# A hybrid transformer block on one core: the first half's small fp32 products become pairs of rounded products

## The chip, the cores and the metric

The kernel runs on one core of a Trainium2 chip. The metric is the device time of one execution, in microseconds; the time before is the median of three runs. A further execution was recorded by the hardware profiler, and everything said of engines, waits and single instructions comes from it.

## The reference

One layer of an encoder trunk for 256 tokens of width 2048, all in float32. Cut to what matters here:

```
u    = rms_norm(x) * g1
proj = u @ w_in                      # q,k,v of two attentions | r,k,v, low-rank inputs of RWKV-7 | three gates
y_a  = stick_breaking_attention      # 4 heads x 128: exp(log_beta + strictly later sums of log(1 - beta)) @ v
y_b  = forgetting_attention          # 4 heads x 128: softmax(q k / sqrt(d) + c[t] - c[s]) @ v, c = cumsum(log f)
y_c  = rwkv7_time_mix                # 16 heads x 64: decay and rate from low-rank products, normalised keys,
                                     # a recurrence over time, group norm, bonus sum(r k r_k) v, gate sigmoid(gd) @ g_up
m    = sum_i sigmoid(gate_i) * (y_i @ P_i)
x    = x + rms_norm(m @ w_out) * g2
x    = x + rms_norm(relu(rms_norm(x) @ w_up)^2 @ w_down) * g4
```

## The kernel before

**Rounded parts.** Weights and activations of the large products are each split in two: a high part in fp32r (a rounded float32, the type that the profile's rows name fp32r) and a low part, the value less the high part. ScalarE writes the high part (`whi`, L152) and VectorE the low one (`wlo`, L153) for each block of 128 x 1024 weights that SP's queue brings in; `split` does the same for an activation, into a tile `pk` of 512 columns, high and low side by side. A large product is then high weights by both activation parts, and low weights by the high part: L168, L172, L176 in `unit` and L198, L214 in `tok`. The small products of the attentions and of RWKV are done in plain fp32.

**Order.** TensorE's instructions stand in an order written out by hand for the first half of the kernel, up to the fourth block of the product with w_out. The main stream runs through the weights of w_in, of the branches and of w_out. Beside it run threads (`mixers`, `gate_norm`, `turns`), Python generators that yield the number of microseconds after which their next piece may be put in. `tick` counts the stream's time with 0.227 us per product of 512 columns and puts in what is due. So a yield decides behind which products of the stream a side product stands. The order on VectorE, ScalarE and POOL is chosen by a scheduler, which keeps each tile's dependences; each engine then works in that order. Tiles with the same tag share `bufs` buffers; a new tile waits until the last use of the one that it takes the place of.

**The threads.** `mixers` does the stick-breaking attention (`sb_mix`), the forgetting attention (`fox_mix`), the activation of the low-rank inputs (`rwkv_lora`) and two halves of RWKV with four head pairs each (`rwkv_half`). A half has these pieces: norm of the keys by a product with `bones`, the block matrix of ones (L543); for each head pair the low-rank products (L567, L569), the decay's running sum, the products within a chunk (L613), the bonus (L619); an inverse of 32 triangular 64 x 64 matrices on VectorE (31 steps, L657 and L659) and two products to finish it (L672, L679); and the passage over four chunks (L698 to L740). `gate_norm` then normalises the result with another product with `bones` (L766), an inverse root, and multiplies by the gate's low-rank product (L779, L780). Side products write to four psum banks `mps`, the stream to four banks `gps`.

**From the first half to the second.** After the product with w_out come the sums of squares of the result for both halves of the tokens (L969), the inverse root (`rstd_of`, L939 and L940 on POOL), the residual sum x1 (L956), its transposes (L988) and their split with a gain into the inputs of the up product (L233 on ScalarE, L234 on VectorE). The squares of x1 for the next norm are summed by ScalarE in `post` of the first eight units of the up product (L1113). `rstd_of` is used once more at the end of the kernel, ahead of the last sum (L1352) and the write of the output.

Of the kernel before, what the change touches and what calls it, by code (L numbers as in the profile page):

```python
# [50 lines left out]
def hybrid_block(ctx, tc, xt, x, gains, params, consts, lora, gup, wst, out):  # L51
# [264 lines left out]
    rstd = rp.tile([128, T], F32, tag="cs", name="rstd1", bufs=1)  # L316
# [41 lines left out]
    def sb_mix():  # L358
        yield "sb"
        q, k, v = done["sbq"], done["sbk"], done["sbv"]  # L360
        B = rp.tile([128, 2, 4, 384], F32, tag="SC", name="sbt", bufs=1)
        z, t = B[:, 0], B[:, 1]
        m0 = rp.tile([128, 4, 384], F32, tag="b6", name="sbm", bufs=1)
        for h in range(4):
# [11 lines left out]
        A.activation(t, t, AF.Ln, bias=1.0)  # L376
        for hp in range(2):
# [6 lines left out]
            yield 5.0 if hp == 0 else 8.0  # L384
        for hp in range(2):
            ps = mps()
            for i in range(2):
                h = 2 * hp + i
                PE.matmul(ps[:, i * 256:i * 256 + 256], C("trig"), z[:, h, 0:256], start=True, stop=False)
                PE.matmul(ps[:, i * 256 + 128:i * 256 + 256], C("ones"), z[:, h, 256:384], start=False, stop=True)  # L390
            V.tensor_tensor(m0[:, 2 * hp:2 * hp + 2, 0:256], ps.rearrange("p (a b) -> p a b", a=2),
                            t[:, 2 * hp:2 * hp + 2, 0:256], ALU.add)
            if hp == 0:
                yield 4.0
        ps = mps()
        PE.matmul(ps.rearrange("p (a b) -> p a b", a=4), C("trig"), z[:, :, 256:384], start=True, stop=True)
        V.tensor_tensor(m0[:, :, 256:384], ps.rearrange("p (a b) -> p a b", a=4), t[:, :, 256:384], ALU.add)
        yield 3.0
        for hp in range(2):
            hs = slice(2 * hp, 2 * hp + 2)  # L400
            A.activation(m0[:, hs], m0[:, hs], AF.Exp)
            for h in (2 * hp, 2 * hp + 1):
                for c in (0, 256):
                    G.tensor_tensor(m0[:, h, c:c + 128], m0[:, h, c:c + 128], C("mst"), ALU.mult)
            yield 2.0 if hp == 0 else 5.0
        out = []
        for h in range(4):
            ps = mps()
            PE.matmul(ps[:, 0:256], v[0][:, h * 128:h * 128 + 128], m0[:, h, 0:256], start=True, stop=False)
            PE.matmul(ps[:, 128:256], v[1][:, h * 128:h * 128 + 128], m0[:, h, 256:384], start=False, stop=True)  # L410
# [7 lines left out]
    def fox_mix():  # L418
# [16 lines left out]
        V.tensor_tensor_scan(lf, one, m0, 0.0, ALU.mult, ALU.add)  # L435
        yield 9.0
# [7 lines left out]
        for hp in range(2):  # L444
            ps = mps()
            for i in range(2):
                PE.matmul(ps[:, i * 256:i * 256 + 256],
                          C("ident", R, 32 + 2 * hp + i, 33 + 2 * hp + i).to_broadcast([4, 128]), lf,
                          start=True, stop=True)
# [58 lines left out]

    def rwkv_lora():
        yield "lora"  # L510
        xl, sy, zz = done["zx"], done["zy"], done["zz"]
        A.activation(xl[0:64], xl[0:64], AF.Tanh)
# [3 lines left out]
        yield 3.0  # L516

    def rwkv_half(hf):
        PR = range(4 * hf, 4 * hf + 4)
        xl, sy, sz = done["zx"], done["zy"], done["zz"]  # L520

# [5 lines left out]
        def lora_load(p):  # L527
            if p in PR:
                lor[p] = rp.tile([128, 128], F32, tag="lor", name=nm("lor"), bufs=2)
                nc.scalar.dma_start(out=lor[p], in_=lora[:, p * 128:p * 128 + 128])  # L530
# [6 lines left out]
        yield 2.6  # L537
        sq = []
        for i2 in range(2):
            ri = B6[:, 2 * i2:2 * i2 + 2, :]  # L540
            ps = mps()
            for i in range(2):
                PE.matmul(ps[:, i * T:i * T + T], C("bones"), rin[2 * i2 + i], start=True, stop=True)  # L543
# [19 lines left out]
        At, Bt, Kt, bon = {}, {}, {}, {}  # L563
        ecol = rp.tile([128, 4, 4], F32, tag="ecol", name=nm("ecol"), bufs=2)
        for i, p in enumerate(PR):
            ps = mps()
            PE.matmul(ps[:, 0:T], lor[p][0:64], xl[0:64], start=True, stop=True)  # L567
            ps2 = mps()
            PE.matmul(ps2[:, 0:T], lor[p][64:128], xl[64:128], start=True, stop=True)  # L569
            lora_load(p + 1)  # L570
            lw = rp.tile([128, T], F32, tag="lw", name=nm("lw"), bufs=1)
            c = rp.tile([128, T], F32, tag="cs", name=nm("cs"), bufs=1)
            th = rp.tile([128, T], F32, tag="tha", name=nm("tha"), bufs=1)
            em = rp.tile([128, T], F32, tag="em", name=nm("em"), bufs=1)
# [7 lines left out]
            A.activation(ep[:, :, 1:65], c4, AF.Exp)  # L582
            A.activation(em, c, AF.Exp, scale=-1.0)
# [20 lines left out]
            V.scalar_tensor_tensor(kp, r, P("rk", p), kp, ALU.mult, ALU.mult)  # L604
            yield f"v{p}"
# [13 lines left out]
            PE.matmul(psb[:, 0:T], C("bones"), kp, start=True, stop=True)  # L619
# [34 lines left out]
        for s in range(31):  # L654
# [5 lines left out]
            yield 0.6 + n * m * 4e-3  # L660
# [81 lines left out]
        start(gate_norm(hf, y, bon, sy, sz))  # L742

    def gate_norm(hf, y, bon, sy, sz):
        PR = range(4 * hf, 4 * hf + 4)
        gqs = {}

        def gup_load(p):
            if p in PR:
                gqs[p] = gq = rp.tile([128, 2, 128], F32, tag="gup", name=nm("gup"), bufs=2)  # L750
                G.memset(gq[:, 1, :], 0.0)
                nc.scalar.dma_start(out=gq[:, 0, :], in_=gup[0:128, 128 * p:128 * p + 128])
                nc.scalar.dma_start(out=gq[0:32, 1, :], in_=gup[128:160, 128 * p:128 * p + 128])

        gup_load(PR[0])
        var = rp.tile([128, 4, T], F32, tag="XT", name=nm("gn"), bufs=2)
# [722 lines left out]
```

## Time and profile before

| | |
|---|---|
| median of three runs | 1534.03 us (1532.95 to 1536.06) |
| profiled execution | 1534.53 us |
| its span, first to last instruction | 1532.8 us |
| mean granted clock of TensorE | 0.995 |
| TensorE's idle time within the span | 29.6 us |

The span lies 1.7 us below the time of the same execution. A line of the groups names the source line, the engine, the operation, the tiles and shapes, and the count; behind the bar stand the busy time in microseconds and the mean duration of one in nanoseconds, and then the idle time ahead of it with what ended it. A line of the timeline begins with the start and the time to the end of the group, both in microseconds. A window gives the busy time of TensorE, its weight loads, VectorE, ScalarE and POOL in that stretch, then the granted clock and the share of the DMA engines. Products overlap in TensorE's pipeline, so the duration of one is longer than its share of the engine's time.

### The profile page before, as it was taken

The page shows a single profiled execution, that of the slowest core. Times are in us where ns is not written, and L with a number is a line of the kernel's source. Part 1 is how long each engine was busy: PE and PEld are TensorE (multiplying, and loading weights), DVE is VectorE, ACT ScalarE, POOL GpSimd, SP SyncE. Part 2 cuts the span into 40 slices and gives each one's busy share as a digit, 9 for nine tenths or more (in the row PEclk, how much of TensorE's full clock was granted, in tenths as well). Part 3 has the DMA queues.
Part 4 walks back from the last instruction along what each step waited for, and adds up shares of the span by engine and source line. Part 5 has one row for each costly group of instructions (what it writes and reads, how often), then busy time and mean ns, then how long its engine had stood idle before and what let it go on. Part 6 is the DMA issues. An engine that isn't in the chain of part 4 may idle for free.

```text
span 1532.8 us, 22383 instructions
## 1 busy us (share of the span) xinstructions
PE 1503.2 (98%) x8294; PEld 1262.6 (82%) x8294; DVE 1192.7 (78%) x1608; ACT 917.8 (60%) x1340; POOL 91.0 (6%) x163
## 2 busy tenths in 40 slices
PE   7999999999999999999999999999999999999997
PEld 6888888888777788778888788888888888888885
DVE  6865567789548789447755868989899999899986
ACT  6664566554546553555444767777667776676753
POOL 0021000000000100000000000000000000000000
PEclk9999999999999999999999999999999999999998
DMA  7555445445534445535695657888888888888974
GB/s 259 192 166 166 164 165 181 165 150 183 182 111 150 165 152 184 175 124 179 208 322 187 231 181 222 249 263 239 262 253 258 242 254 270 249 246 264 260 247 151
DMA packets 105117, 316.88 MB, mean 207 GB/s; under 512 B 10288, under 2 KB 12720, under 8 KB 104624
## 3 DMA queue, kind: packets, MB, share of 16 engines
q1 hardware_dynamic: 93536, 282.76, 54.1%
q0 software_dynamic: 8064, 29.36, 10.3%
q10 hardware_dynamic: 3408, 3.34, 0.6%
q8 instruction: 65, 1.06, 0.3%
q14 instruction: 44, 0.36, 0.1%
HBM read 281.86 MB, written 4.19 MB: 187 GB/s over the span
## 4 chain that ended last, share of the span: by engine, by line
PE 53%; DVE 1%; DMA 1%; ACT 1%; issue 0%; POOL 0%; DVEq 0%; POOLq 0%; ACTq 0%
PE gps L168 14%; PE gps L214 10%; PE gps L172 8%; PE mps L1209 3%; PE mps L1210 3%; PE mps L1211 3%; PE gps L198 3%; PE gps L1211 2%; PE gps L1209 2%; PE gps L1210 2%; PE gps L176 1%; DMA sp<-in_wst_dram 1%; DVE x L1352 0%; DVE wlo L153 0%; ACT junk L1113 0%
## 5 line engine op out<-in xcount | busy, mean ns | idle before, releaser
L153 DVE TENSOR_TENSOR wlo<-raw,whi 128x1024 fp32r<-128x1024 f32 x507 | 616.0, 1222 | 192.2 <-ACT whi L152 174.8
L152 ACT ACTIVATE whi<-raw 128x1024 fp32r<-128x1024 f32 x507 | 533.9, 1057 | 276.0 <-PE gps L214 107.7
L168 PE MATMUL gps<-pk,whi 128*128 128x512 f32 x1301 | 330.9, 393 | 0.1
L214 PE MATMUL gps<-whi,pk 128*128 128x512 f32 x1144 | 291.5, 394 | 0.0
L168 PEld LDWEIGHTS gps<-pk,whi 128*128 128x128 f32 x1301 | 241.1, 188 | 48.4 <-issue 0.9
L214 PEld LDWEIGHTS gps<-whi,pk 128*128 128x128 f32 x1144 | 213.7, 188 | 45.8 <-issue 1.0
L172 PEld LDWEIGHTS gps<-pk,wlo 128*128 128x128 f32 x1391 | 190.1, 190 | 14.6 <-issue 1.2
L172 PE MATMUL gps<-pk,wlo 128*128 128x256 f32 x1391 | 195.8, 283 | 0.0
L214 PE MATMUL gps<-wlo,pk 128*128 128x512 f32 x572 | 157.4, 394 | 0.0
L214 PEld LDWEIGHTS gps<-wlo,pk 128*128 128x128 f32 x572 | 106.9, 188 | 23.2 <-issue 0.7
L1075 DVE TENSOR_TENSOR sp<-raw,sp 128x1024 fp32r<-128x1024 f32 x67 | 81.7, 1220 | 4.8 <-ACT sp L1074 4.6
L1074 ACT ACTIVATE sp<-raw 128x1024 fp32r<-128x1024 f32 x67 | 70.7, 1055 | 14.9 <-PE mps L1211 3.9
L1101 ACT ACTIVATE sp<-gps 128x512 f32<-128x512 f32 x52 | 31.1, 597 | 80.7 <-PE gps L176 80.7
L198 PE MATMUL gps<-whi,pk 128*128 128x512 f32 x264 | 71.9, 393 | 0.0
L1209 PE MATMUL mps<-whi,fm 128*128 128x512 f32 x168 | 66.2, 394 | 0.0
L1210 PE MATMUL mps<-whi,fm 128*128 128x512 f32 x168 | 65.8, 392 | 0.0
L1211 PE MATMUL mps<-wlo,fm 128*128 128x512 f32 x168 | 65.5, 390 | 0.0
L1171 POOL DMA_DIRECT2D raw<-raw x40 | 35.0, 874 | 430.8 <-DVE raw L1168 133.4
L198 PEld LDWEIGHTS gps<-whi,pk 128*128 128x128 f32 x264 | 49.3, 188 | 10.6 <-ACT whi L152 0.2
L1211 PE MATMUL gps<-wlo,fm 128*128 128x512 f32 x126 | 49.3, 391 | 0.4 <-DVE wlo L153 0.4
L1209 PE MATMUL gps<-whi,fm 128*128 128x512 f32 x126 | 49.2, 391 | 0.0
L1168 DVE TENSOR_TENSOR raw<-raw,raw 128x1024 f32<-128x1024 f32 x40 | 48.8, 1219 | 0.4
(342 smaller groups left out, 1961.4 us busy)
## 6 DMA issues: line engine op xcount, KB each, us to landing
raw<-in_wst_dram SPq DMA_DIRECT2D x502, 512.0 KB, 4.4
raw<-raw POOLq DMA_DIRECT2D x40, 512.0 KB, 7.3
sp<-in_wst_dram SPq DMA_DIRECT2D x16, 512.0 KB, 5.6
raw<-sp POOLq DMA_DIRECT2D x8, 512.0 KB, 7.7
sp<-raw POOLq DMA_DIRECT2D x8, 512.0 KB, 6.5
x<-in_x_dram SPq DMA_DIRECT2D x8, 256.0 KB, 6.3
xs<-x SPq DMA_DIRECT2D x2, 1024.0 KB, 4.0
x<-xs SPq DMA_DIRECT2D x4, 512.0 KB, 7.4
```

The source lines that it names most:

```text
L152: A.activation(hi, raw, AF.Copy)
L153: V.tensor_tensor(lo, raw, hi.bitcast(F32), ALU.subtract)
L168: PE.matmul(ps, hi[:, i * 128:i * 128 + 128], pks[i], start=first and i == 0, stop=False)
L172: PE.matmul(ps[:, 0:T], lo[:, i * 128:i * 128 + 128], pks[i][:, 0:T], start=False, stop=False)
L198: PE.matmul(ps[tt], pks[k][:, c:c + 128], w[:, (k - k0) * 512:(k - k0) * 512 + 512], start=k == 0 and part == 0 and w is hl[0], stop=w is ...
L214: PE.matmul(ps[tt], pks[k][:, c:c + 128], w[:, (k - k0) * 512:(k - k0) * 512 + 512], start=k == 0 and part == 0 and w is hl[0], stop=False)
L1074: A.activation(hi, raw, AF.Copy)
L1075: V.tensor_tensor(lo, raw, hi.bitcast(F32), ALU.subtract)
L1168: V.tensor_tensor(x, x, z, ALU.add)
L1209: PE.matmul(Q[f], p, w, start=d == 0 and i == 0, stop=False)
L1210: PE.matmul(Q[f], pl, w, start=False, stop=False)
L1211: PE.matmul(Q[f], p, wl, start=False, stop=d == nd - 1 and i == 1)
```

## The change

Small fp32 products of the first half become two or more products in fp32r. The operand with arbitrary values is split into a high part, copied by ScalarE, and a low part, subtracted by VectorE; matrices of ones and zeros (`bones`, `tri`, `pick`) are copied to fp32r once. Products within a chunk, the passage over the chunks, the attention's products with q, k and v and all transposes stay in fp32.

The low-rank weights (`lora`) and the gate's weights (`gup`) are split too. For the low rank, the two products with 64 rows become four with 128 rows: high and low weights stacked on the partitions against the high input, and then against the low input. For the gate, four products take the place of two. Several tiles move to other tags to make room: `c` shares a buffer with `kn`, `em` overwrites `lw`, one of the four buffers `m` holds the low-rank inputs' parts. Yields change: 3.6 more in the stick-breaking attention, 3.0 more in `rwkv_lora`, 1.2 more ahead of the key norm, shorter ones in the triangle's steps, and in `gate_norm` 7.0 and 4.5 (first half) or 5.0 and 2.5 (second) instead of 7.5, and 2.8 instead of 2.0 per head pair in the first half. Between the halves of the kernel, L939 moves from POOL to VectorE, both high parts of a bank are written before both low parts, and the squares of L1113 are written to a psum bank instead of `junk`.

```diff
 def sb_mix():
+        zh = rp.tile([128, 4, 384], F32R, tag="b6", name="sbh", bufs=1)
+        zl = [rp.tile([128, 2, 384], F32R, tag="XT", name="sbl", bufs=2) for _ in range(2)]
+        for hp in range(2):
+            hs = slice(2 * hp, 2 * hp + 2)
+            A.activation(zh[:, hs], z[:, hs], AF.Copy)
+            V.tensor_tensor(zl[hp], z[:, hs], zh[:, hs].bitcast(F32), ALU.subtract)
+        yield 3.6
...
-                PE.matmul(ps[:, i * 256:i * 256 + 256], C("trig"), z[:, h, 0:256], start=True, stop=False)
-                PE.matmul(ps[:, i * 256 + 128:i * 256 + 256], C("ones"), z[:, h, 256:384], start=False, stop=True)
+                for n, zp in enumerate((zh[:, hs], zl[hp])):
+                    PE.matmul(ps[:, i * 256:i * 256 + 256], tri[:, 0], zp[:, i, 0:256], start=i == n == 0, stop=False)
+            for n, zp in enumerate((zh[:, hs], zl[hp])):
+                PE.matmul(ps.rearrange("p (a b) -> p a b", a=2)[:, :, 128:256], tri[:, 1], zp[:, :, 256:384],
+                          start=False, stop=n == 1)
...
-        PE.matmul(ps.rearrange("p (a b) -> p a b", a=4), C("trig"), z[:, :, 256:384], start=True, stop=True)
+        PE.matmul(ps.rearrange("p (a b) -> p a b", a=4), tri[:, 0], zh[:, :, 256:384], start=True, stop=False)
+        for hp in range(2):
+            PE.matmul(ps[:, 256 * hp:256 * hp + 256].rearrange("p (a b) -> p a b", a=2), tri[:, 0],
+                      zl[hp][:, :, 256:384], start=False, stop=hp == 1)
 def fox_mix():
...
-                PE.matmul(ps[:, i * 256:i * 256 + 256],
-                          C("ident", R, 32 + 2 * hp + i, 33 + 2 * hp + i).to_broadcast([4, 128]), lf,
-                          start=True, stop=True)
+                for part in (lh, ll):
+                    PE.matmul(ps[:, i * 256:i * 256 + 256],
+                              pick[:, 2 * hp + i:2 * hp + i + 1].to_broadcast([4, 128]), part,
+                              start=part is lh, stop=part is ll)
 def rwkv_half(hf):
...
+        def lora_split(p):
+            if p in PR:
+                raw = lor[p]
+                A.activation(wl, raw, AF.Copy)
+                for i, r in enumerate((slice(64, 128), slice(0, 64))):
+                    V.tensor_tensor(wl[r, i], raw[r, i], wl[r, i].bitcast(F32), ALU.subtract)
...
-        yield 2.6
-        sq = []
+        sq, sqh = [], []
+        for i2 in range(2):
+            s = B6[:, 2 * i2:2 * i2 + 2, :]
+            hl = [rp.tile([128, 2, T], F32R, tag="BK", name=nm("sqh"), bufs=8) for _ in range(2)]
+            A.activation(hl[0], s, AF.Copy)
+            V.tensor_tensor(hl[1], s, hl[0].bitcast(F32), ALU.subtract)
+            sqh.append(hl)
+        yield 3.8
...
-            for i in range(2):
-                PE.matmul(ps[:, i * T:i * T + T], C("bones"), rin[2 * i2 + i], start=True, stop=True)
+            for n, part in enumerate(sqh[i2]):
+                PE.matmul(ps.rearrange("p (a b) -> p a b", a=2), bones, part, start=n == 0, stop=n == 1)
...
-            PE.matmul(ps[:, 0:T], lor[p][0:64], xl[0:64], start=True, stop=True)
-            PE.matmul(ps2[:, 0:T], lor[p][64:128], xl[64:128], start=True, stop=True)
+            for j, (q, x2) in enumerate(((ps, xw), (ps2, xa))):
+                for n in range(2):
+                    PE.matmul(q[:, 0:T], wl[:, j], x2[n], start=n == 0, stop=n == 1)
...
-            PE.matmul(psb[:, 0:T], C("bones"), kp, start=True, stop=True)
+            PE.matmul(psb[:, 0:T], bones, kph, start=True, stop=False)
+            PE.matmul(psb[:, 0:T], bones, kpl, start=False, stop=True)
...
-            yield 0.6 + n * m * 4e-3
+            yield 0.5 + n * m * 3.2e-3
 def gate_norm(hf, y, bon):
...
+        for i2, ps in enumerate(pss):
+            for n, part in enumerate((hi, lo)):
+                PE.matmul(ps.rearrange("p (a b) -> p a b", a=2), bones, part[:, 2 * i2:2 * i2 + 2], start=n == 0,
+                          stop=n == 1)
...
         rsqrt(ri, var, sc)
-        yield 7.5
+        gup_split(PR[0])
+        gup_split(PR[1])
+        yield 5.0 if hf else 7.0
+        gup_load(PR[2])
+        gup_load(PR[3])
+        yield 2.5 if hf else 4.5
...
-            PE.matmul(ps[:, 0:T], gq[:, 0, :], sy, start=True, stop=False)
-            PE.matmul(ps[:, 0:T], gq[:, 1, :], sz, start=False, stop=True)
+            for n, (j, x2) in enumerate(((0, syh), (0, syl), (2, syh), (1, z3))):
+                PE.matmul(ps[:, 0:T], gr[:, j], x2, start=n == 0, stop=n == 3)
+            gup_split(p + 2)
...
-            yield 2.0
+            yield 2.0 if hf else 2.8
 # rstd_of
-        G.tensor_scalar(r, ss[:, 3:4], 1.0 / D, sums, ALU.mult, ALU.add)
+        V.tensor_scalar(r, ss[:, 3:4], 1.0 / D, sums, ALU.mult, ALU.add)
 # split of the transposes
-            split(trs[k2 // 2][:, i * T:i * T + T], u, P("g3", k2 + i))
+        for i, u in enumerate(us):
+            A.activation(u[:, 0:T], src[i], AF.Copy, scale=P("g3", k2 + i))
+        for i, u in enumerate(us):
+            V.scalar_tensor_tensor(u[:, T:], src[i], P("g3", k2 + i), u[:, 0:T].bitcast(F32), ALU.mult, ALU.subtract)
 # post of an up unit
-                A.activation(junk(), x1[j % 2][:, 512 * (j // 2):512 * (j // 2) + 512], AF.Square,
+                A.activation(ps[0], x1[j % 2][:, 512 * (j // 2):512 * (j // 2) + 512], AF.Square,
```

More of the change, by code (lines that the diff above doesn't have):

```diff
@@ L360, in sb_mix @@
         q, k, v = done["sbq"], done["sbk"], done["sbv"]
-        B = rp.tile([128, 2, 4, 384], F32, tag="SC", name="sbt", bufs=1)
-        z, t = B[:, 0], B[:, 1]
+        W = rp.tile([128, 16 * 256], F32, tag="SC", name="sbt", bufs=1)
+        z, t = (W[:, 1536 * i:1536 * i + 1536].rearrange("p (a b) -> p a b", a=4) for i in range(2))
         m0 = rp.tile([128, 4, 384], F32, tag="b6", name="sbm", bufs=1)
+        zh, zl = [], []
         for h in range(4):
@@ L507, in hybrid_block @@
     yc = [None] * 8
+    bones = rp.tile([128, 128], F32R, name="bones")
+    syh, syl, z3 = (rp.tile([128, T], F32R, name=n) for n in ("syh", "syl", "z3"))
     def rwkv_lora():
@@ L528, in lora_load @@
             if p in PR:
-                lor[p] = rp.tile([128, 128], F32, tag="lor", name=nm("lor"), bufs=2)
-                nc.scalar.dma_start(out=lor[p], in_=lora[:, p * 128:p * 128 + 128])
+                lor[p] = rp.tile([128, 2, 128], F32, tag="lor", name=nm("lor"), bufs=1)
+                for r in (0, 64):
+                    nc.scalar.dma_start(out=lor[p][r:r + 64], in_=lora.rearrange("(s r) c -> r s c", s=2)
+                                        [:, :, p * 128:p * 128 + 128])
+        def lora_split(p):
[4 more added lines that the diff above has]
+                    V.tensor_tensor(wl[r, i], raw[r, i], wl[r, i].bitcast(F32), ALU.subtract)
         lora_load(PR[0])
@@ L563, in rwkv_half @@
         At, Bt, Kt, bon = {}, {}, {}, {}
+        lora_split(PR[0])
         ecol = rp.tile([128, 4, 4], F32, tag="ecol", name=nm("ecol"), bufs=2)
@@ L582, in rwkv_half @@
             A.activation(ep[:, :, 1:65], c4, AF.Exp)
+            em = lw
             A.activation(em, c, AF.Exp, scale=-1.0)
```

108 lines of the change are left out of this document (75 added, 33 removed).

## The prediction

> **What bounds the kernel now.** I read the page first, then the groups by line with shapes kept apart, the timeline of the places where TensorE works for the first half's side jobs, the list of waits, and the windows.
>
> ```profile
> span 1532.8 us, 22383 instructions
> PE 1503.2 (98%) x8294; PEld 1262.6 (82%) x8294; DVE 1192.7 (78%) x1608; ACT 917.8 (60%) x1340; POOL 91.0 (6%) x163
> ...
> 100.00:705.00 605.00, 601.58 (x3762) 498.07 (x3761) 421.91 (x642) 320.99 (x499) 31.73 (x79) 1.00 0.49 163
> ```
>
> TensorE works 1503.2 of 1532.8 us, and 601.6 of 605 in the stretch of the page's time (100 to 705 us) that holds nearly all the changed products. There VectorE is busy 421.9 us and ScalarE 321.0, so 183 and 284 us are free on them. The stream of weight products is never short of work in that stretch, so a microsecond taken from TensorE's side jobs ends the run a microsecond sooner, as long as the new vector work fits into the free time.
>
> **Price of a product.** The mean of a row is one product's latency; what counts is the distance between starts.
>
> ```profile
> 275.20 1.11 PE L172 MATMUL gps<-pk,wlo 128*128 128x256 f32 x8
> 276.15 0.40 PE L176 MATMUL gps<-pk,whi 128*128 128x512 f32 x1
> 276.38 2.00 PE L168 MATMUL gps<-pk,whi 128*128 128x512 f32 x8
> 278.22 1.11 PE L172 MATMUL gps<-pk,wlo 128*128 128x256 f32 x8
> ...
> 459.17 1.89 PE L543 MATMUL mps<-b,con 128*128 128x256 f32 x8
> ```
>
> Rounded (fp32r) products: eight of 256 columns take 276.15 - 275.20 = 0.95 us, 0.119 each; eight of 512 take 278.22 - 276.38 = 1.84, 0.230 each. The eight fp32 instructions of L543 end 1.89 us after their first start; less the last one's latency (0.379, row below) that is seven distances, 0.216 each.
>
> ```profile
> L619 PE MATMUL mps<-g,con 128*128 128x256 f32 x16 | 4.8, 380 | 0.0
> L543 PE MATMUL mps<-b,con 128*128 128x256 f32 x16 | 3.8, 379 | 0.0
> L766 PE MATMUL mps<-gn,con 128*128 128x256 f32 x16 | 3.8, 378 | 0.0
> L779 PE MATMUL mps<-zy,gup 128*128 128x256 f32 x16 | 5.1, 403 | 2.0 <-DVE g L781 2.0
> L780 PE MATMUL mps<-zz,gup 128*128 128x256 f32 x16 | 5.2, 410 | 0.0
> L389 PE MATMUL mps<-sbt,con 128*128 128x256 f32 x8 | 2.4, 379 | 0.0
> L447 PE MATMUL mps<-foxf,ident 4*128 4x256 f32 x8 | 2.0, 384 | 0.0
> L390 PE MATMUL mps<-sbt,con 128*128 128x128 f32 x8 | 1.5, 273 | 0.0
> L396 PE MATMUL mps<-sbt,con 128*128 128x512 f32 x2 | 1.0, 594 | 0.0
> ```
>
> Each fp32 product of the code stands here as two instructions (L543: eight in the code, sixteen in the row), so it costs 0.43 us at 256 columns; two rounded products in its place cost 0.24.
>
> **The products, part by part.** Key norm (L543): 16 x 0.216 = 3.46 us; after, per half, two pairs of 512 columns, 8 x 0.230 = 1.84. Saved 1.6. Gate norm (L766): the same, 1.6. Bonus (L619): 3.46 against 16 x 0.119 = 1.90. Saved 1.6. Gate products (L779, L780): 32 x 0.216 = 6.91 against four rounded ones for each of eight head pairs, 32 x 0.119 = 3.81. Saved 3.1. Forget sums (L447): 8 x 0.216 = 1.73 against 0.95. Saved 0.8. Triangle: L389 gives 8 x 0.216 = 1.73; L390 has half the columns and a latency 0.106 shorter, so 8 x 0.11 = 0.88; L396 has twice the columns and 0.215 more, so 2 x 0.43 = 0.86; together 3.47. After: 14 rounded ones of 256 columns and one of 512, 1.90. Saved 1.6.
>
> Low rank (L567, L569) needs a look of its own:
>
> ```profile
> 271.80 1.11 PE L172 MATMUL gps<-pk,wlo 128*128 128x256 f32 x8
> 272.84 0.48 PE L567 MATMUL mps<-zx,lor 64*128 64x256 f32 x1
> 272.85 0.48 PE L569 MATMUL mps<-zx,lor 64*128 64x256 f32 x1
> 273.16 0.38 PE L567 MATMUL mps<-zx,lor 64*128 64x256 f32 x1
> ...
> 273.47 1.89 PE L168 MATMUL gps<-pk,whi 128*128 128x512 f32 x7
> ```
>
> The two products of 64 rows start together, but the second pair starts 0.32 us later and the next work 0.31 after that. Before them eight products should end at 272.75 (8 x 0.119 from 271.80), so the switch costs 0.09; behind them seven take 275.20 - 273.47 = 1.73 instead of 7 x 0.230, another 0.12. That is 0.84 us for the pair, about two products in turn. After: four rounded ones with all 128 rows, 0.48. Saved 8 x 0.36 = 2.9. [...]
>
> Sum of the products: 1.6 + 1.6 + 1.6 + 3.1 + 0.8 + 1.6 + 2.9 = 13.2 us.
>
> **The stall at 480 us.** It is the longest wait of TensorE between its start and the passage.
>
> ```profile
> 480.15 0.50 PE L214 MATMUL gps<-wlo,pk 128*128 128x512 f32 x1
> 482.64 0.95 PE L779 MATMUL mps<-zy,gup 128*128 128x256 f32 x2 [1.99 <-DVE g L781]
> ...
> 484.68 2.79 PE L214 MATMUL gps<-whi,pk 128*128 128x512 f32 x8
> ...
> 482.17 0.42 DVE L781 TENSOR_TENSOR g<-mps,g 128x256 f32<-128x256 f32 x1
> ```
>
> The third gate product needs a psum bank that the first gives back in L781, and VectorE comes to L781 late, behind the inverse root of gate_norm and the key norm of the next half. From 480.15 to 482.64 are 2.49 us where 0.23 would do: 2.3 lost. Then the clock is down: eight products take 2.79 us instead of 2.00 (0.8), the four instructions of L779 and L780 and the one before about 1.1 more. In all 4.2. The change moves gate_norm(0) later in TensorE's order: 11.5 us behind the root instead of 7.5, and 2.8 instead of 2.0 per head pair, so the third product stands 5.6 us later. Added to VectorE ahead of L781 are four subtractions of 512 columns and some small ones, about 4 us. I take 3.5 of the 4.2, with the ends 0 (stall as before) and 4.2. [...]
>
> **What is added on the other engines.**
>
> ```profile
> L231 DVE TENSOR_TENSOR pk<-tmp,pk 128x256 fp32r<-128x256 f32 x16 | 6.2, 413 | 0.0
> L1142 DVE TENSOR_TENSOR fm<-sfm,fm 128x512 fp32r<-128x512 f32 x28 | 19.2, 685 | 1.1 <-ACT fm L1136 1.1
> L230 ACT ACTIVATE pk<-tmp 128x256 fp32r<-128x256 f32 x16 | 6.3, 412 | 2.5 <-DVE tmp L338 2.4
> 474.97 0.44 ACTq L753 DMA_DIRECT2D gup<-in_gup_dram  x1
> ```
>
> VectorE: eight subtractions of 512 columns (key and gate norm) 5.5 us; thirteen of 256 (bonus, low rank's inputs, forget sums) 5.4; two of 768 some 2; 32 of 128 columns or less (lora_split, gup_split), each under 0.41, about 9: 22 us in all, 12% of its free 183. ScalarE: about 45 copies at 0.4 to 0.7, some 23 us, and 24 more DMA issues (lora twice instead of once, gup four times instead of twice per head pair) at up to 0.44, 10 us: 12% of its free 284. SP's queue gets nothing, POOL loses four scalar operations and clears less. So the throughput is there; what remains is local lateness. I charge 1.0 us for small new waits; the ends are 0 and one more stall like that at 480, 4.2. If the cover of one pair of splits were gone, TensorE would wait out a copy and a subtraction, 0.7 + 0.7 us each time. The shorter triangle yields change nothing: its vector work runs ahead of them and TensorE's next product of that chain is far behind. The lows take one of four m buffers until the last low-rank product at 538 us; the fourth m is first written at 569, so nothing waits.
>
> ```profile
> 538.10 0.38 PE L569 MATMUL mps<-zx,lor 64*128 64x256 f32 x1
> 568.98 0.67 DVE L875 SCALAR_TENSOR_TENSOR m<-th,gps 128x512 f32<-128x512 f32 x1
> ```
>
> **Passage and end.**
>
> ```profile
> 842.91 0.86 POOL L939 TENSOR_SCALAR rs<-ss,ssum 128x1 f32<-128x1 f32 x1 [1.97 <-ACT junk L969]
> 844.98 1.97 PE L988 MATMUL mps<-ident,x 128*128 128x128 f32 x8 [1.81 <-DVE x L956]
> ...
> 844.40:854.50 10.10, 7.93 (x37) 5.33 (x38) 9.85 (x22) 7.73 (x23) 0.01 (x1) 0.83 0.63 248
> ...
> PE mps L988 <- DVE pk L234: 1.6, 4, 0.5
> ...
> 1512.86 0.20 DVE L936 TENSOR_SCALAR ssum<-ssum,eps 128x1 f32<-128x1 f32 x1
> ...
> 1524.55 0.76 POOL L939 TENSOR_SCALAR rs<-ss,ssum 128x1 f32<-128x1 f32 x1 [4.29 <-ACT junk L1338]
> ```
>
> L939 goes from POOL (0.76 to 0.86 us) to VectorE (0.20). At the end of the kernel it lies on the path: 0.76 - 0.20 = 0.5 saved, or nothing if VectorE's product with the gain (L1341) is put ahead of it. In the passage VectorE is still at the first token half's sums when the second's sum of squares is done, so the gain is between 0 and 0.7. The eight squares of x1 (L1113), which now go into a psum bank of the up product, leave the passage on ScalarE; that and the order of the two high parts free ScalarE, but VectorE is busy 9.85 of 10.10 us there, and it stays. I take 0.8 us for the passage. Ends: -1.0 (an estimate: the scalar operation queued behind one vector pass over 512 columns, 0.69 in L1142, with its handover) and +3.1 (0.7 from L939, 0.8 of the 1.97 that the eight transposes take at half clock, and the four waits of the following rounds, 1.6).
>
> **Sum.** 13.2 + 3.5 + 0.8 + 0.5 - 1.0 = 17.0 us. The profiled execution took 1534.5 us (1.7 beyond its span), so 1517.5; the median shown is 1534.0, 0.5 below, which would give 1517.0. I keep 1517.5.
>
> **Rivals.**
> *New waits eat part of it.* Splits stand on two engines between data and product, each in a queue with the weight splits; the stall at 480 stays and a second one of its kind comes with gate_norm(1) or the key norm. 13.2 + 0.8 + 0.5 - 1.0 - 4.2 = 9.3: 1525. For it: that stall was just such a queue. Against it: the longer yields. 0.17.
> *The low rank saves nothing:* the old pair, started together, costs the stream one product of 0.43, because other work fills the rest, and the new form 0.48. 8 x 0.05 lost instead of 2.9 gained: 3.3 less, 1520.8. For it only the common start. 0.08.
> *The passage gives all,* with no drop of the clock: 2.3 more, and no new waits, 1.0: 1514. Against it VectorE's 9.85. 0.12.
> *The freed time isn't used:* each product ends sooner, but the weight splits can't follow and TensorE waits for wlo instead. Then 13.2 shrinks to 2 or 3 and the time is about 1530. For it that many splits land just ahead of their use; against it VectorE's free 183 us. 0.07.
> *Slower.* One mechanism: em now overwrites lw, and c shares one buffer with kn, so kn waits for the second exponential, then POOL's two products, then L613.
>
> ```profile
> 489.78 0.87 POOL L603 TENSOR_TENSOR Bt<-g,ep 128x256 f32<-128x256 f32 x1
> 497.38 1.16 PE L613 MATMUL mps<-Bt,At 64*128 64x128 f32 x16
> ```
>
> If TensorE waited at L613 in each of eight head pairs, at 4.2 us (a wait of 2.3 and the clock), that is 34 us: 1551. It decides from four such stalls on. Against it: POOL ends at 490.65 and L613 starts at 497.38, 6.7 us of slack for half a microsecond of added chain. 0.06.
> The forecast itself keeps 0.50.
>
> **Numbers.** Change smaller than 0.2% (3.1 us) can hardly be told from none. Faster: forecast, low rank, passage, new waits, 0.87, and a third of the unused case: 0.89; within: 0.06; slower 0.05. The range leaves out the slower and the unused case and some of the edges: 1512.5 to 1526.
>
> **What would show it.** TensorE's busy time near 1490 us with the share about the same; the products with bones, the gate's and the low rank's 0.12 (256 columns) or 0.23 us (512) from start to start; no wait of the gate's products for VectorE and no half clock between 470 and 490 us; L939 on VectorE. Wrong if TensorE's idle time in the first 700 us grows by more than 5 us, or if the rounded pairs stand further apart than 0.12 us.

## The result and the profile after

The changed kernel takes 1525.67 us (median of four runs, 1523.48 to 1526.64), the kernel before 1533.88 beside it: a ratio of 0.9942 (95% interval 0.9929 to 0.9954), 8.2 us less. The forecast was 17.0 us less, 1517.5. The time lies at the upper end of the range, 0.3 us inside it, so half of the expected gain is missing, and the question is where it went.

The page of the changed kernel, engines over the whole span (busy time, share, instructions):

```profile
span 1524.9 us, 22504 instructions
PE 1492.9 (98%) x8275; PEld 1257.4 (82%) x8275; DVE 1213.8 (80%) x1667; ACT 935.2 (61%) x1390; POOL 88.3 (6%) x159
```

VectorE has 21.1 us more work, where the forecast had 22, and ScalarE 17.4, where it had 23. TensorE has 10.3 us less, and 32.0 us of idle time instead of 29.6.

**The products cost what the forecast said.** The timeline of TensorE in the changed kernel:

```profile
449.43 1.07 PE L605 MATMUL mps<-sqh,bones 128*128 128x512 f32 x4
450.33 0.62 PE L214 MATMUL gps<-whi,pk 128*128 128x512 f32 x2
450.79 1.07 PE L847 MATMUL mps<-gn,bones 128*128 128x512 f32 x4
...
474.01 0.52 PE L633 MATMUL mps<-lows 128*128 128x256 f32 x3
...
474.48 0.63 PE L214 MATMUL gps<-wlo,pk 128*128 128x512 f32 x2
...
476.80 0.28 PE L869 MATMUL mps<-syh,gup 128*128 128x256 f32 x1
...
477.26 0.63 PE L214 MATMUL gps<-wlo,pk 128*128 128x512 f32 x2
```

From start to start: the key norm's four take 450.33 - 449.43 = 0.90 us, the gate norm's four stand in a row of the same length, the low rank's four 474.48 - 474.01 = 0.47, the gate's four 0.46. That is 0.23 each at 512 columns and 0.12 at 256, as counted.

**Where the rest went.** The waits of TensorE between 440 and 500 us, with what released them (us in total, times, longest):

```profile
PE gps L214 <- DVE wlo L153: 4.0, 1, 4.0
PE mps L688 <- DVE g L871: 1.6, 1, 1.6
```

The wait of the gate's product at 480 us (2.0 us on L779) is gone, but a wait of twice that length stands 17 us earlier, for a weight low. The timeline around it, all three engines:

```profile
460.03 1.04 ACT L152 ACTIVATE whi<-raw 128x1024 fp32r<-128x1024 f32 x1
...
461.09 1.28 ACT L239 ACT_TABLE_LOAD   x1
...
462.38 1.06 ACT L239 ACTIVATE gn<-gn 128x1024 f32<-128x1024 f32 x1
...
463.48 1.23 DVE L240 TENSOR_TENSOR gn<-gn 128x1024 f32<-128x1024 f32 x1 [2.69 <-ACT gn L239]
464.62 0.68 DVE L622 TENSOR_TENSOR b<-b 128x512 f32<-128x512 f32 x1
465.22 1.22 DVE L241 TENSOR_TENSOR gn<-gn,gn 128x1024 f32<-128x1024 f32 x1
466.36 1.22 DVE L153 TENSOR_TENSOR wlo<-raw,whi 128x1024 fp32r<-128x1024 f32 x1
...
467.63 2.07 PE L214 MATMUL gps<-wlo,pk 128*128 128x512 f32 x4 [3.99 <-DVE wlo L153]
469.50 2.76 PE L214 MATMUL gps<-whi,pk 128*128 128x512 f32 x6
```

The high part that L153 needs was written at 460.03 + 1.04 = 461.07. But L153 stands in VectorE's queue behind three operations: L240 of gate_norm's inverse root, L622 of the next half's key norm, and L241. L240 waits for ScalarE, which first loads a function table (1.28 us) and computes L239. VectorE idles 2.69 us with the weight split ready behind it, and L153 starts 5.3 us after its input was there. TensorE's last product before it began at 463.25, so 4.38 us pass where 0.23 would do: 4.15 lost. Then the clock is at half until 473.25 (windows below): six products take 472.06 - 469.50 = 2.56 us, 0.427 each, and of the 5.6 us from 467.63 to 473.25 some 2.6 are lost. Together 6.8 us. With the wait of the bonus product L688 for a psum bank (1.6) that is 8.4 us where the stall before cost 4.2 by the forecast's count.

The start of the same weight product in both kernels gives the whole account. Gain against the kernel before in us, one profiled execution each, counted from weight product 400 (ahead of the first change) up to product 1600 (333 us, half of the small products), 3200 (767 us, all of them), 3600 (behind the passage), 4800 (1142 us) and the last of 6232 that write to `gps`. The rows below the first are runs of the next section:

| kernel | 1600 | 3200 | 3600 | 4800 | last |
|---|---|---|---|---|---|
| changed | 5.3 | 8.4 | 9.2 | 9.2 | 7.1 |
| weight lows first | 5.3 | 8.2 | 9.3 | 9.3 | 8.0 |
| products alone | 5.3 | 8.2 | 8.3 | 8.3 | 7.7 |
| passage edits alone | 0.0 | 1.6 | 3.3 | 3.3 | 2.1 |
| second half later | 5.4 | 12.6 | 14.4 | 14.4 | 15.1 |
| second half later, gate spread | 5.3 | 15.4 | 16.8 | 16.8 | 13.0 |
| the same again | 5.3 | 15.2 | 16.2 | 16.2 | 16.2 |
| the same, old low rank | 3.9 | 12.4 | 13.5 | 13.5 | 13.4 |
| gate norm later | 5.3 | 6.0 | 6.4 | 6.4 | 3.4 |
| gate on POOL | 5.3 | 4.0 | 5.6 | 5.6 | 5.6 |
| kernel before, same pauses | 0.0 | -1.0 | -1.7 | -1.7 | -2.2 |

For the changed kernel: 13.2 from the products, 4.2 from the old stall and 8.4 to the new ones would be 9.0; measured are 8.4. (With 3.9 for the old stall, its price by the clock windows at the end, it would be 8.7.) The passage adds 0.9 (0.8 forecast), the end 0.5 (0.5 forecast: 11.5 us from the end of the last product to the end of the span became 11.0). In the second half of the kernel 2.1 us are given back in small waits. 8.4 + 0.9 - 2.1 + 0.5, and 0.3 ahead of product 400, make 8.0, beside the 7.9 us between the two profiled executions (1534.53 and 1526.64).

### The profile page after: what moved, and what is told of

Read it like the earlier page. It is cut to its first block, busy times and chain, and to the rows that moved or that the text cites. A ratio compares the mean times of both kernels' runs of the same rounds, so it can differ in the third digit from the quotient of the medians.

```text
span 1524.9 us, 22504 instructions
## 1 busy us (share of the span) xinstructions
PE 1492.9 (98%) x8275; PEld 1257.4 (82%) x8275; DVE 1213.8 (80%) x1667; ACT 935.2 (61%) x1390; POOL 88.3 (6%) x159
## 4 chain that ended last, share of the span: by engine, by line
PE 53%; DVE 1%; issue 1%; DMA 1%; ACT 0%; POOL 0%; POOLq 0%; DVEq 0%; SPq 0%; ACTq 0%
PE gps L168 14%; PE gps L214 10%; PE gps L172 8%; PE mps L1304 3%; PE mps L1302 3%; PE mps L1303 3%; PE gps L198 3%; PE gps L1304 2%; PE gps L1302 2%; PE gps L1303 2%; PE gps L176 1%; DVE wlo L153 1%; DMA sp<-in_wst_dram 1%; PE mps L993 0%; DVE raw L1261 0%
## 5 line engine op out<-in xcount | busy, mean ns | idle before, releaser
L153 DVE TENSOR_TENSOR wlo<-raw,whi 128x1024 fp32r<-128x1024 f32 x507 | 617.0, 1224 | 169.2 <-ACT whi L152 154.8
L172 PEld LDWEIGHTS gps<-pk,wlo 128*128 128x128 f32 x1391 | 189.9, 190 | 13.4 <-DVE wlo L153 0.2
L1167 ACT ACTIVATE sp<-raw 128x1024 fp32r<-128x1024 f32 x67 | 70.6, 1054 | 16.8 <-PE mps L1303 4.9
```

The costliest lines, as they stand in the source:

```text
L153: V.tensor_tensor(lo, raw, hi.bitcast(F32), ALU.subtract)
L172: PE.matmul(ps[:, 0:T], lo[:, i * 128:i * 128 + 128], pks[i][:, 0:T], start=False, stop=False)
L1167: A.activation(hi, raw, AF.Copy)
```

## The experiments

Two theories at first. A: the products give 13 us, and one meeting on VectorE takes back the rest. B: the pairs of rounded products give only some 8 us.

**Weight lows first.** The subtraction of a weight's low part is put up to 50 places ahead in VectorE's order, in the changed kernel and in the kernel before (first half only).

```diff
-        V.tensor_tensor(lo, raw, hi.bitcast(F32), ALU.subtract)
+        with tc.high_priority(offset=50):
+            V.tensor_tensor(lo, raw, hi.bitcast(F32), ALU.subtract)
```

> The changed kernel, with the low-part subtraction of the weights (wlo) raised in priority for the first half, so that VectorE's order has it ahead of the inverse root of gate_norm(0) where both are open; the same work. Theory A (the products give their 13 us, and one stall ate the rest: VectorE's order had the root, which waits for ScalarE, ahead of a wlo that was ready, TensorE stood 4.15 us at 463 us and then ran 6.8 us at half clock): the wait at 463 us and the half clock go, 4.1 + 3.4 = 7.5 us, so about 1518 us (1516 to 1521). Theory B (the pairs of rounded products give only some 8 us, the stall stands where TensorE had room anyhow): 1524 to 1526, with other waits in the stall's place.

> The kernel before with the same priority for wlo: the control for e1. The wait of the third gate product at 480 us was for L781, not for wlo, so both theories leave it or make it longer: 1530 to 1535 us. The difference to e1 is what theories differ in: A expects 12 to 14 us, B about 8.

Measured: the changed kernel 1525.84 us (0.9942, 0.993 to 0.9955), the kernel before 1535.42 (1.0007, 0.9998 to 1.0015). No gain in either. The control is 0.4 us beyond what was expected of it. The times alone would speak for B, the 9.6 us between the two as well. The waits of TensorE between 440 and 500 us in the first (lines are about six higher here: L692 transposes, L694 the bonus, L875 the gate's products) say otherwise:

```profile
PE mps L692 <- DVE g L877: 3.0, 1, 3.0
PE mps L875 <- DVE gup L837: 1.2, 1, 1.2
PE mps L694 <- ACT Kt L701: 0.8, 1, 0.8
PE mps L875 <- DVE gup L836: 0.7, 1, 0.7
```

The wait of 4.0 us for the weight low is gone; what was put behind it, the gate's splits and the product that returns a psum bank, is now late by as much. VectorE shows why. The window from 460 to 490 us (columns: TensorE, weight loads, VectorE, ScalarE, POOL, clock, DMA share, GB/s) of the kernel before:

```profile
460.00:490.00 30.00, 28.01 (x117) 22.44 (x117) 26.20 (x42) 21.02 (x28) 3.03 (x9) 0.94 0.44 148
```

The same window of the changed kernel:

```profile
460.00:490.00 30.00, 25.36 (x121) 20.28 (x119) 26.12 (x45) 17.95 (x29) 3.62 (x9) 0.89 0.40 131
```

And of the changed kernel with the lows first:

```profile
460.00:490.00 30.00, 23.73 (x121) 18.61 (x120) 28.00 (x47) 18.58 (x28) 4.37 (x9) 0.99 0.52 167
```

VectorE was busy 26.2 of these 30 us before the change, and 28.0 with the lows first. So little is free that putting one operation first makes another late. Whether the work as such is too much for this stretch these rows don't show; the spread version below says that it is not.

**Parts alone.** The changed kernel without its three edits to the passage and the end (L1029 on VectorE, both high parts first, the squares into a psum bank); and the kernel before with only these three.

> The changed kernel without the three edits behind the first half (L939 on VectorE, both high parts first, squares of x1 into a psum bank). Compared at the same product of the stream the passage gave 0.9 us, the end 0.5, and 2.1 us were lost at five places of the second half between 1190 and 1350 us. Theory A: if the passage's edits caused those waits, 1525.7 + 1.4 - 2.1 = 1525 us; theory B': if the waits come from the stream standing elsewhere against the transfers, 1527 us.

> The kernel before with those three edits alone. Passage 0.9 and end 0.5 us faster: 1532.5 us if the second half keeps its order; about 1534.6 if the edits themselves bring the five small waits (2.1 us) of the second half.

Measured: products alone 1528.4 us (0.9963, 0.995 to 0.9976), the three edits alone 1531.24 (0.9982, 0.9974 to 0.9991). Against 1534.66 for the kernel before on that chip, 6.3 and 3.4 us. Both expectations were missed: the first is slower than either of its two values, the second faster. In the profiled executions, the table gives the three edits alone 1.7 us in the passage (3.3 - 1.6); the 1.6 us ahead of it have another cause, the clock, below. In the second half of the kernel the products alone lose 0.6 us, the edits alone 1.2 and the changed kernel 2.1, so these waits belong to neither part by itself.

**The meeting taken apart.** If the meeting of root and key norm on VectorE is the cause, it can be moved by a pause in the threads, without touching a product.

```diff
 def rwkv_half(hf):
         lora_load(PR[0])
+        if hf:
+            yield 8.0
```

> The second half of RWKV (its key norm and everything behind it) begins 8 us of the stream later; nothing else differs from the changed kernel. Theory A (the key norm of the second half and the inverse root of gate_norm of the first half meet on VectorE at 451 to 475 us, and its in-order queue then holds back the weight lows that TensorE waits for): the wait of L214 at 463 us (4.0 us of idle and 6.8 us at half clock, 6.9 us lost) falls below 2 us, and a part of the later waits stays: 1518 to 1521 us. Theory B (the room on the other engines is used up, so a stall moved in one place comes back in another, here at the end of the first half, where the branch waits for gate_norm of the second): 1524 to 1527 us.

Measured 1521.05 us (0.9919, 0.9903 to 0.9934), at the upper edge of A's range. The wait for the weight low is down from 4.0 to 1.1 us and there is no half clock in this place (granted clock 1.00 from 440 to 500 us). Left between 440 and 500 us are:

```profile
PE gps L198 <- ACT whi L152: 1.2, 1, 1.2
PE gps L214 <- DVE wlo L153: 1.1, 1, 1.1
PE gps L198 <- DVE wlo L153: 1.1, 1, 1.1
```

The other side of the meeting, with gate_norm of the first half 12 us later instead:

```diff
 def gate_norm(hf, y, bon):
+        if not hf:
+            yield 12.0
```

> gate_norm of the first half begins 12 us of the stream later, the second half of RWKV as in the changed kernel. Theory A: the meeting at 451 to 475 us is taken apart from the other side, so the wait of L214 at 463 us goes, but the root and the gate's products now meet the first two head pairs on VectorE: 1518 to 1523 us. Theory B: 1524 to 1527 us.

Measured 1527.43 us (0.9959, 0.9946 to 0.9972): outside what A said, and 0.4 beyond B. The wait at 463 us is gone, but root and gate now meet the first head pairs, and that is worse:

```profile
487.20 1.19 PE L682 MATMUL mps<-Bt,At 64*128 64x128 f32 x7 [7.61 <-DVE At L660]
```

Both together with more room: the second half 8 us later, and the gate's products spread.

```diff
-        yield 2.5 if hf else 4.5
+        yield 2.5 if hf else 8.5
...
-            yield 2.0 if hf else 2.8
+            yield 2.0 if hf else 6.0
```

> As the kernel with the second half 8 us later, and the gate's products of the first half begin 4 us later and stand 6.0 us apart instead of 2.8. Theory A: neither the wait at 463 us nor those at 473 to 491 us are left: 9.3 us lost between 440 and 500 us become 1 or less, 1516 to 1518 us. Theory B: 1523 to 1527 us.

> The kernel with the second half 8 us later and the gate's products spread once more, beside the two others on the same chip: 1518 to 1521 us, whatever the theory; its trace shows whether the waits of the second half of the kernel (3.8 us given back between 1190 and 1350 us) come again: if they depend on each execution's transfers they move or go, if on the order of the instructions they stay where they were.

Measured 1519.66 us (0.9905, 0.9888 to 0.9921), and again 1517.67 (0.9893, 0.9879 to 0.9906). The first is 1.7 us above A's range and 3.3 below B's; the second is 0.3 below what was expected of it. This version is faster than both kernels. Between 440 and 500 us its second execution has one wait. The list of waits and the window:

```profile
PE mps L871 <- ACT Kt L697: 1.1, 1, 1.1
```

```profile
440.00:500.00 60.00, 58.88 (x298) 47.96 (x297) 48.94 (x79) 44.90 (x68) 4.37 (x11) 1.00 0.50 161
```

TensorE works 58.9 of 60 us. The same window of the changed kernel has 54.4, and the clock at 0.94:

```profile
440.00:500.00 60.00, 54.41 (x268) 44.35 (x267) 47.24 (x77) 40.44 (x65) 4.86 (x13) 0.94 0.43 142
```

By product 3200 it has gained 15.4 and 15.2 us; the forecast's terms for this part were 13.2 + 3.5 - 1.0 = 15.7. So the products give what their starts say, and B is out: the missing 7 us were the meeting on VectorE.

So it was a matter of order more than of room. The stretch from 460 to 490 us in the same execution:

```profile
460.00:490.00 30.00, 30.00 (x151) 24.28 (x150) 27.75 (x49) 22.73 (x33) 3.97 (x9) 1.00 0.47 149
```

VectorE is busier here than in the changed kernel (27.75 against 26.12 of 30 us), since the stream gets further, and yet TensorE never stops. The gate norm's products stand where they stood, behind weight product 2028; the key norm's come behind product 2062 instead of 2026, so the two inverse roots follow each other in VectorE's queue instead of taking turns: gate norm's L243 ends at 465.00 us, and the key norm's first operation (L619 here) starts at 464.92.

**Two operations to POOL, same pauses.** Two of five vector operations per head pair of gate_norm run on POOL.

```diff
-            V.tensor_tensor(y[p], y[p], ri[:, i, :], ALU.mult)
+            G.tensor_tensor(y[p], y[p], ri[:, i, :], ALU.mult)
...
-            V.tensor_tensor(y[p], y[p], bon[p], ALU.add)
+            G.tensor_tensor(y[p], y[p], bon[p], ALU.add)
```

> Two of the five vector operations per head pair of gate_norm (the product with the inverse root and the sum with the bonus) run on POOL; order and pauses as in the changed kernel. Theory A: VectorE's queue is shorter only behind the root, so the wait of L214 at 463 us stays (the root and the key norm are not touched) and the 1.6 us of L688 for the psum bank shrinks: 1523.5 to 1526 us. If plain occupation of VectorE were the cause, whatever the order, 3.4 us less of it would show as up to 3.4 us: 1522 us.

Measured 1527.8 us (0.9962, 0.9949 to 0.9975), worse than either said. The wait at 463 us stays, as A had it, and TensorE waits twice more for weight lows:

```profile
PE gps L214 <- DVE wlo L153: 6.8, 3, 4.0
```

But this run hardly makes VectorE's work less. Over the whole span its busy time falls from 1213.8 to 1212.7 us, although sixteen operations of about 0.41 us left it. The timeline shows POOL's work and VectorE's beside it:

```profile
469.27 6.39 POOL L863 TENSOR_TENSOR g<-g,gn 128x256 f32<-128x256 f32 x4 [23.42 <-DVE gn L243]
474.98 1.23 DVE L622 TENSOR_TENSOR b<-b 128x512 f32<-128x512 f32 x1
476.24 1.86 DVE L831 TENSOR_TENSOR gup<-gup,gup 32x128 fp32r<-32x128 f32 x1
```

L622 takes 1.23 us beside POOL's work and 0.68 or 0.69 in the three other places of this trace, where POOL is idle; L831 takes 1.86 us here and 0.28 alone. What VectorE saved, operations that ran beside POOL's took back, so the run decides nothing between order and occupation.

**Low rank as before.** In the spread version, the low-rank products with one load, no splits, and two fp32 products of 64 rows.

```diff
-                for n in range(2):
-                    PE.matmul(q[:, 0:T], wl[:, j], x2[n], start=n == 0, stop=n == 1)
+            PE.matmul(ps[:, 0:T], lor[p][0:64], done["zx"][0:64], start=True, stop=True)
+            PE.matmul(ps2[:, 0:T], lor[p][64:128], done["zx"][64:128], start=True, stop=True)
```

> The kernel with the second half 8 us later and the gate's products spread, with the low-rank products as in the kernel before: one load of the weights, no split of them, two fp32 products of 64 rows in place of four rounded ones of 128. By the starts in the traces (0.84 us a pair before, 0.47 for the four after) the first half is 2.9 us longer than with the rounded ones, less what the spared splits free: 1522 to 1523 us beside 1519.7. By the rival (the pair costs what one product costs, 0.43) it is the same or 0.4 us shorter: 1519.3 us.

Measured 1522.65 us (0.9923, 0.9909 to 0.9938), within what was expected, 5.0 more than the spread version beside it. The table is sharper: 1.4 us less gain at product 1600 (four pairs done) and 2.8 at 3200 (all eight), 0.35 a pair. The forecast had 0.36. By the rival, in which the old pair costs what one product costs (0.43), this term would be an estimated -0.4. The measurement decides against it, for 2.8.

**The same pauses in the kernel before.**

```diff
 def rwkv_half(hf):
+        if hf:
+            yield 8.0
...
-        yield 7.5
+        yield 7.5 if hf else 15.5
...
-            yield 2.0
+            yield 2.0 if hf else 6.0
```

> The kernel before with the same pauses: second half 8 us later, the gate's products of the first half 8 us later and 6.0 us apart. Theory A (all products together save 13 us, the rest is stalls): the stall at 480 us (2.3 us and, in some executions, 1.9 more at half clock) goes and nothing else changes: 1530 to 1532 us, so the products and the passage are worth 10.5 to 14 us against the spread kernel. Theory B (the products are worth only some 8 us, and the rest of the spread kernel's gain is the pauses): 1526 to 1528 us.

Measured 1536.08 us (1.0012, 1.0003 to 1.0021): neither. The wait at 480 us is gone, but between 590 and 720 us TensorE waits for gate weights and for a weight low:

```profile
PE mps L782 <- DMA gup<-in_gup_dram: 2.0, 1, 2.0
PE gps L198 <- DVE wlo L153: 1.7, 1, 1.7
```

So the pauses alone gain nothing in the old kernel. And this run gives the price of the products by itself, from TensorE's busy time between weight products 400 and 3200. The granted clock is 1.00 in both rows, so busy time is taken as work. This kernel first, then the spread version, second execution:

```profile
91.00:776.50 685.50, 680.02 (x4142) 563.45 (x4141) 474.30 (x711) 359.98 (x552) 34.07 (x82) 1.00 0.51 168
...
90.90:760.10 669.20, 666.88 (x4122) 556.66 (x4121) 494.04 (x764) 378.18 (x598) 32.12 (x84) 1.00 0.52 173
```

That is 13.1 us less work on TensorE, where the forecast's sum was 13.2. The kernel before with the three edits alone (mean clock of its span 0.997) is busy 679.4 us in this part, which would make it 12.5.

## Why the prediction was half right

**The products, 13.2 us: right.** Gain at product 1600, where half of the key norm, bonus and low rank and all of the triangle and the forget sums are done: 0.8 + 0.8 + 1.45 + 1.6 + 0.8 = 5.45 by the forecast's terms, 5.3 to 5.4 measured in all eight traces that have these products in full. The whole, by TensorE's busy time, is 12.5 to 13.1.

**The stall, 3.5 us saved: this step failed.** It was judged at its own place: the third gate product moves back by 5.6 us, about 4 us of work come ahead of it on VectorE, so it fits. That was so; the gate's third product no longer waits there. What it left out is that the two roots move too: the products of the key norm and the gate norm stand behind weight products 2026 and 2028 instead of 2040 and 2044, so the roots meet other weight splits in VectorE's queue, and L240 held up a split behind it while it waited 2.69 us for ScalarE. (In the kernel before L240 stood ahead of a split too, but TensorE did not wait for that one.) The term came out at -4.2 (4.2 before, 8.4 after) in place of +3.5. Of the signs named beforehand, "no half clock between 470 and 490 us" failed, since the half clock lasts until 473.25. The sign of being wrong, more than 5 us of new idle time in the first 700 us, did not show the failure: idle time grew only from 13.4 to 16.6 us, since TensorE counts as busy for 5.62 of the 6.83 us at half clock.

**"12% of its free 183 us": the argument that allowed it.** The free time was counted over 605 us. In the 30 us from 460 to 490 VectorE was busy 26.2 of 30 in the kernel before, so 3.8 us were free there, and that row was to be had before the change was made. It would have been a warning and no more: the spread version has 2.25 us free there and no wait. What decided was which operation stood ahead of the split.

**Small waits, 1.0 us: right only in the first 330 us.** There nothing is lost: the gain at product 1600 is the products' own. In the stretch of the stall they are part of the term above; behind the passage 2.1 us more were given back.

**The rivals.** The one that came true is the first, "new waits eat part of it", at 0.17: it gave 1525 by a second stall of the old kind. Its time is right and its mechanism nearly so: one stall of twice the length, and 1.6 us more on a psum bank. The range held the result, by 0.3 us, because it took in this rival; the forecast's own account of the stall did not happen. It deserved more than a third of the forecast's 0.50. The low rank that saves nothing, the freed time that isn't used, and the slower case are excluded by the rows above; no wait on L613's successor L682 shows in the changed kernel.

**Passage and end, 1.3 us: right by the trace (0.9 and 0.5), for partly other reasons.** L1029 on VectorE takes 0.20 us in place of POOL's 0.76 to 0.86, but in the passage it stands behind four residual sums, so it gains nothing there:

```profile
832.39 2.74 DVE L1046 SCALAR_TENSOR_TENSOR x<-mg,rs,x 128x512 f32<-128x512 f32 x4
...
835.04 0.20 DVE L1029 TENSOR_SCALAR rs<-ss,ssum 128x1 f32<-128x1 f32 x1
...
836.46 0.72 PE L1078 MATMUL mps<-ident,x 128*128 128x128 f32 x3 [1.88 <-DVE x L1046]
```

What came of it is the waits of the following rounds (L988 for `pk`, 1.6 us in four before), which are gone from the list after. The size of this term stays open: 0.9 us here, 1.7 with the three edits alone.

**The second half of the kernel.** Its 2.1 us were not foreseen, and nothing shows that they come of the change: the spread version gave back 3.8 us there in one execution and nothing in the next, with the same program. In the first, the longest of these waits is for a high part that ScalarE writes into `sp`, and POOL at that time waits for the load of the weights in `sp`:

```profile
1322.54 0.87 POOL L1266 DMA_DIRECT2D raw<-sp  x1 [12.48 <-DMA sp<-in_wst_dram]
...
1323.17 0.50 PE L1304 MATMUL mps<-sp,fm 128*128 128x512 f32 x1 [1.14 <-ACT sp L1169]
```

The second execution has the same load released earlier:

```profile
1320.62 0.87 POOL L1266 DMA_DIRECT2D raw<-sp  x1 [11.93 <-DMA sp<-in_wst_dram]
```

That is 1.92 us earlier. At product 4800 the first execution was 1.57 us ahead of the second; by the product before this wait it is 0.32 us behind, so about half of the 3.8 us went in smaller waits on the way. Against the stream, then, the load came 1.92 - 0.32 = 1.6 us later, and behind this wait the first execution is 1.92 us behind. That points to the transfers here; why they differ from one execution to the next, and whether they explain the rest, stays open.

## What to carry to other kernels

Free time on an engine does not tell whether new work will fit: 183 us free in 605 hid a stretch with 3.8 of 30 free, and even there the work fitted once its order was right, with 2.25 of 30 free and no wait. When work for a queue like VectorE's here is made longer or moved, look for what waits inside that queue (L240, 2.69 us, for a function table and an exponential on ScalarE) with something urgent behind it (L153, 5.3 us late); putting the urgent work first only made the next one late, taking the two chains apart gave the gain back. A time inside the forecast's range is no proof of the parts: the gain at the same product of the stream, kernel against kernel, showed which term had failed. And where POOL took over work here, operations of VectorE beside it took longer (L622 1.23 us instead of 0.68), so the durations on both engines are to be read afterwards.

## What the runs showed of the hardware

**Half clock, and the idle time ahead of it.** The kernel before is at half clock from 482.95 to 486.36 us, from 844.76 to 848.18, and from 1524.01 to the end of the span, where TensorE has no product left (0.00 us busy). The changed kernel is at half clock from 466.42 to 473.25, from 838.47 to 841.88, and from 1517.70 to the end. The rows below are windows of 3.41 or 3.42 us. The changed kernel around 463 us:

```profile
463.01:466.42 3.41, 0.63 (x3) 0.19 (x1) 2.94 (x4) 2.33 (x3) 0.00 (x0) 1.00 0.00 1
466.42:469.83 3.41, 2.20 (x5) 1.81 (x6) 3.41 (x6) 0.00 (x0) 0.06 (x1) 0.50 0.36 111
469.83:473.25 3.42, 3.42 (x11) 2.84 (x11) 3.42 (x5) 0.05 (x1) 1.04 (x2) 0.50 0.36 119
473.25:476.66 3.41, 3.41 (x18) 2.82 (x17) 2.83 (x7) 2.93 (x6) 0.20 (x1) 1.00 0.68 231
```

The kernel before around 480 us:

```profile
479.53:482.95 3.42, 1.43 (x7) 0.77 (x7) 3.42 (x8) 2.32 (x4) 1.11 (x3) 1.00 0.24 42
482.95:486.36 3.41, 3.41 (x9) 2.64 (x8) 3.41 (x6) 2.64 (x6) 0.20 (x1) 0.50 0.70 262
```

The passage edits alone around 478 us:

```profile
477.92:481.33 3.41, 1.94 (x9) 0.86 (x7) 3.41 (x7) 1.66 (x2) 1.35 (x3) 1.00 0.32 121
481.33:484.74 3.41, 2.89 (x13) 2.44 (x14) 3.41 (x9) 2.98 (x7) 0.21 (x1) 1.00 0.64 183
```

The spread version, first execution, at 1321 us:

```profile
1320.86:1324.27 3.41, 1.91 (x8) 0.92 (x6) 1.11 (x1) 2.20 (x3) 0.87 (x1) 1.00 0.67 247
1324.27:1327.69 3.42, 3.25 (x16) 2.79 (x17) 3.42 (x6) 2.49 (x5) 0.00 (x0) 1.00 0.71 134
```

In these rows, one with TensorE busy 1.43 of 3.42 us is followed by one at half clock; one with 0.63 of 3.41 by two, the first of them busy 2.20; after 1.91 and 1.94 the clock stays at 1.00. The kernel before and the one with the passage edits alone have the same gap ahead of L779 (2.49 and 2.50 us from start to start, TensorE idle 1.99 in both). In the first, 3.41 us at half clock followed and 1.6 us more were lost; in the second, the clock stayed at 1.00. That is the 1.6 us of the table's fourth row; the three edits lie behind this place. So this gap cost some 2.3 us in one execution and 3.9 in the other, and its length alone did not tell which. The busy time of a window alone did not either. In the kernel before with the pauses it is 2.06 us from 844.37, and half clock follows:

```profile
844.37:847.78 3.41, 2.06 (x10) 1.10 (x10) 2.69 (x8) 1.58 (x5) 0.69 (x2) 1.00 0.75 308
847.79:851.20 3.41, 2.64 (x10) 2.02 (x9) 3.36 (x10) 3.41 (x13) 0.00 (x0) 0.50 0.01 2
```

What brings the clock down is not shown by these runs.
